# A two-layer hybrid trunk on one core: warm opening, low parts last, GpSimd for some low parts, another norm and pump order

## The chip, the cores and the metric

The kernel runs on one core of a Trainium2 chip, as one program. The metric is the device time of one execution in microseconds (us), and of several runs the median. Engines: PE (TensorE), whose matmuls bear the work; DVE (VectorE), ACT (ScalarE) and POOL (GpSimd) for work on elements; SP, which issues most DMAs. All of them run side by side, each through its own queue in order, and wait for each other through semaphores. TensorE's granted clock is given as a share of its full 2.4 GHz; the lower level is 1.2 GHz, shown as 0.50.

## The reference

Two layers over 256 positions of 1024 channels, all in float32, with a conditioning vector c that gives each layer shifts, scales and gates:

```python
for l in range(2):
    mod = silu(c) @ ada_w[l] + ada_b[l]           # 6 x 1024: shift, scale, gate, twice
    h = rmsnorm(x) * norm_mix * (1 + sc1) + sh1
    proj = h @ w_in[l]                            # one projection, split by columns
    # c_q, c_kv, k_rope | q, k, v, o, i, f of the mLSTM | two merge gates
    y_mla  = attention(rmsnorm(c_q) @ w_uq, rmsnorm(c_kv) @ w_ukv, rope)   # block-causal
    y_lstm = sigmoid(o) * headnorm(mlstm(silu(conv(q, k)), v, i, f))       # running maximum M
    x = x + g1 * ((sigmoid(g_a) * (y_mla @ w_bra) + sigmoid(g_l) * (y_lstm @ w_brl)) @ w_out)
    h = rmsnorm(x) * norm_ffn * (1 + sc2) + sh2
    a, v = split(conv3(h @ w_up))                 # 2816 channels each
    x = x + g2 * ((gelu(a) * v) @ w_down)
return rmsnorm(x) * final
```

## The kernel before

Activations lie with channels on the 128 partitions and the 256 positions along the free axis. A weight matrix is read in units, most of them 1024 x 256, and a unit in two pieces of 128 x 1024, each one DMA of 512 KB on SP's queue into `raw`. Float32 accuracy is reached by splitting: `_Weights.split` lets ACT copy a piece to the high part `whi` (fp32r) and DVE subtract it to get the low part `wlo`, and activations are split in the same way (`hh` and `hl`, `mh` and `ml`, `gh` and `gl`, `ua` and `ub`). A product is then three matmuls per 128 x 128 block of weights: high by high, high by low activation, low by high activation; `fm_steps` and `tm_steps` issue these three for each k in turn, and with `late_lo` all low weight parts of a slot behind the others.

The program is emitted unit by unit. A unit takes its weights with `W.take()`, which also loads further ones and queues the split of the next; `pair_slots` makes its four slots of 12 matmuls. Between slots `unit` advances side generators (evictions, norms, attention and mLSTM pieces, each yielding between its steps), emits one queued split piece, and, where a list of slots says so, a pump: `ada_block` reads 512 KB of ada_w on SP's queue and multiplies it on DVE by silu(c), summing along the row. So where a DVE operation stands in its queue is set by the slot at which it was emitted. The lists are `BRANCH_PUMPS` (units of the two branch projections), `OUT_PUMPS`, `UP_PUMPS` and `DOWN_PUMPS`; `NORM_AT` is the unit of the down projection at which the next layer's scales are put together. Each operation on ACT and DVE is also held back by `_Engine` until the one eight before it is emitted as done, so the order hardly shifts; all are recorded on one or two lines of its helper.

The stages of the trace, in us: the opening (0 to 52) with the first norm and the first six units of w_in's columns, block by block as x's blocks are normalised; the rest of the projection with the norms of c_q and c_kv, w_uq and w_ukv (to 115); attention and mLSTM between more units (to 178.5); the branch projections w_bra and w_brl (to 202.5), out (to 244), up (to 360), down (to 402), then the second layer the same way.

In the opening, GpSimd raises the mean square to the power −1/2 (`rs_cols`), `rs_tile` broadcasts it over partitions with matmuls and ACT copies it to `rs`, by which DVE multiplies x.

Of the kernel before, what the change touches and what calls it, by code (L numbers as in the profile page):

```python
# [19 lines left out]
P = 128  # L20
T = 256
# [39 lines left out]
BRANCH_PUMPS = (0, 2, 4, 6)  # L61
OUT_PUMPS = ((1, 2, 3, 4, 5), ())
UP_PUMPS = ((4, 6, 8), ())
DOWN_PUMPS = ((2, 2, 2, 2, 2, 1, 1, 1, 1, 1, 1), (1,) * 8)
NORM_AT = 11
# [6 lines left out]
MASK_SLOTS = (4, 3) + (2,) * 6  # L72
LATER = (2, 2, 2, 0)
# [5 lines left out]
class _Part:  # L79


    def __init__(self, nk, m):
        self.nk, self.m, self.cut, self.tiles = nk, m, (nk + 1) // 2, []
# [10 lines left out]
class _Weights:  # L94


    def __init__(self, nc, act, dve, raw, hi, lo, nm, ahead):
        self.act, self.dve = act, dve
# [5 lines left out]
    def add(self, src, nk, m):  # L104
        self.list.append((src, nk, m))
# [7 lines left out]
    def split(self, r):  # L113
# [5 lines left out]
        self.dve.tensor_tensor(l, r, h.bitcast(F32), ALU.subtract)  # L119
        return h, l  # L120

    def load_to(self, n):
        while self.loaded < min(n, len(self.list)):
            src, nk, m = self.list[self.loaded]
            part = _Part(nk, m)
            c0 = 0
            for i in range(2):
                c = part.cols(i)
                part.tiles.append(self.load(src[:, c0:c0 + c]))
                c0 += c  # L130
# [3 lines left out]
    def queue_split(self, n):  # L134
# [4 lines left out]
        src, nk, m = self.list[n]  # L139
# [3 lines left out]
        def piece(i):  # L143
            def emit():
                h, l = self.split(raw.tiles[i])
# [4 lines left out]
        self.pieces += [piece(0), piece(1)]  # L150
# [42 lines left out]
def hybrid_trunk(ctx, tc, a):  # L193
# [48 lines left out]
    W = _Weights(nc, act, dve, wraw, whi, wlo, nm, ahead=2)  # L242
# [48 lines left out]
    def tm_steps(out, w, h, ks, tb, csl, start=True, stop=True):  # L291
# [4 lines left out]
        for i, k in enumerate(ks):  # L296
# [4 lines left out]
            pe.matmul(out, hh[:, k, tsl], wl.at(k, csl), start=False, stop=last)  # L301
# [89 lines left out]
    dve.memset(minus_half, -0.5)  # L391
    halfpi = const.tile([P, 1], F32, name="halfpi")
# [114 lines left out]
    def norm_columns(n, l, wkey, sh, sc):  # L507
# [10 lines left out]
        for b in n.filled:  # L518
            u_fill(n, b)

# [37 lines left out]
    def norm_rest(n):  # L558
# [10 lines left out]
        for k0 in range(0, KB, 2):  # L569
# [10 lines left out]
            yield  # L580
# [26 lines left out]
    def mixer(l, n, begun):  # L607
# [26 lines left out]
        ats = sA.tile([8, T], F32, name=nm("ats"), tag="ats")  # L634
# [8 lines left out]
        def c_evict(i0, srcs):  # L643
# [5 lines left out]
            for i, src in enumerate(srcs):  # L649
                b = i0 + i  # L650
                gain = ppc(l, "qn", b) if b < 3 else ppc(l, "kvn", b - 3)
                if begun:
# [53 lines left out]
        def gates():  # L706
# [52 lines left out]
            dve.tensor_copy(ats, at[0:8, :T])  # L759
            dve.tensor_tensor_scan(M, ats, ats, 0.0, ALU.max, ALU.max)  # L760
# [234 lines left out]
        if begun:  # L995
# [7 lines left out]
            W.flush()  # L1003
            next(misc)
            for c in cs:
                next(c)
            sides.extend([conv, misc] + cs[1:] + cs[:1] + [widen()])
        else:
# [6 lines left out]
            slots, outs = pair_slots(W.take(), h, [bank()[:, :T], bank()[:, :T]])  # L1015
# [4 lines left out]
        for i in range(4):  # L1020
            if 3 + i not in first:
                slots, outs = pair_slots(W.take(), h, late_lo=bool(first) and i == 1)
# [24 lines left out]
        for hp in range(2):  # L1047
            b = bank()

            def slot(b=b, hp=hp):  # L1050
                for j in range(2):
                    fm_steps(b[:, j * T:(j + 1) * T], w, (ch[0], cl[0]), range(2),
                             slice((2 * hp + j) * P, (2 * hp + j + 1) * P), h0=3)
# [3 lines left out]
        for tb in range(2):  # L1057
            b = bank()

            def slot(b=b, tb=tb):  # L1060
                tm_steps(b, w, ckv, range(2), tb, slice(512, 1024))
# [104 lines left out]
    def ffn(l, fx, n):  # L1166
# [3 lines left out]
        def evict(j, srcs):  # L1170
# [6 lines left out]
            yield  # L1177
# [16 lines left out]
        for j in range(FB):  # L1194
# [5 lines left out]
            slots, outs = pair_slots(W.take(), h, [bank()[:, :T], bank()[:, :T]] if j == 2 else None)  # L1200
# [36 lines left out]
    for l in range(DEPTH):  # L1237
# [76 lines left out]
    normalised(slice(0, 1))  # L1314
    for k in range(KB):
# [11 lines left out]
        for dst in (h32, hh):  # L1327
# [178 lines left out]
```

## Time and profile before

| | before |
|---|---|
| runs | 814.19, 814.35 (the median), 817.71 us |
| the profiled execution, its own time | 819.43 us |
| its span in the trace | 817.6 us |
| busy: PE, DVE, ACT, GpSimd | 786.3, 687.1, 497.9, 91.7 us |
| bytes moved by DMA | 188.67 MB, 231 GB/s on the mean |

The span is the time from the first to the last event of the profiled execution, and its own time includes what lies around that. PE is close to always busy, so the reader should look less at the shares than at what fills the gaps in PE's row of the timeline, stage by stage. "128x1024" is partitions by elements; `wlo<-raw,whi` reads: the low part is written from raw and the high part. In the rows by stage the engines stand in the order PE, PEld (weight loads), DVE, ACT, POOL, each with its count of instructions. A bracket at the end of a timeline row is idle time of that engine just before the operation, and what ended it.

### The profile page before, as it was taken

How to read it: one execution, taken by the hardware profiler on the slowest of the kernel's cores; microseconds unless marked ns; L12 is line 12 of the kernel's file. 1: busy time of each engine (PE TensorE's matmuls, PEld its weight loads, DVE VectorE, ACT ScalarE, POOL GpSimd, SP SyncE). 2: the span in 40 equal slices, each digit the busy share in tenths (PEclk: the TensorE clock that was granted, in tenths of full speed). 3: DMA queues.
4: the chain of work that ended last, by engine and by line, in shares of the span. 5: the costliest groups of instructions: out<-in, count | busy, mean ns of one | idle time of the engine just before them, and what ended most of it. 6: DMA issues, size and time to landing. Idle time of an engine off the chain costs nothing. (4 is left out here: it accounts for less than half of the span.)

```text
span 817.6 us, 16692 instructions
## 1 busy us (share of the span) xinstructions
PE 786.3 (96%) x6416; PEld 769.2 (94%) x6416; DVE 687.1 (84%) x1244; ACT 497.9 (61%) x912; POOL 91.7 (11%) x118
## 2 busy tenths in 40 slices
PE   5999899999999999999899998999999999999995
PEld 4999789999899999999899998999999999999995
DVE  6979888789999988898968887788987988889742
ACT  5657658644577666643557584866366866665541
POOL 5801232000100000000101022100011000000010
PEclk7999999999999999999999998999999999999998
DMA  9986896788847755478876479677864565646841
GB/s 338 397 293 185 251 337 205 249 299 279 263 144 252 246 195 194 126 251 289 308 289 200 132 231 330 212 230 246 303 224 156 181 218 176 196 138 210 285 120 51
DMA packets 57712, 188.67 MB, mean 231 GB/s; under 512 B 6896, under 2 KB 8992, under 8 KB 57632
## 3 DMA queue, kind: packets, MB, share of 16 engines
q1 hardware_dynamic: 55520, 183.10, 66.6%
q0 software_dynamic: 1248, 2.28, 1.1%
q10 hardware_dynamic: 864, 2.23, 0.8%
q8 instruction: 50, 0.82, 0.4%
q14 instruction: 30, 0.25, 0.1%
HBM read 184.29 MB, written 1.06 MB: 227 GB/s over the span
## 5 line engine op out<-in xcount | busy, mean ns | idle before, releaser
L184 ACT CAST whi<-raw 128x1024 fp32r<-128x1024 f32 (+3 forms) x276 | 259.7, 950 | 120.0 <-PE bank L184 74.7
L184 DVE TENSOR_TENSOR wlo<-raw,whi 128x1024 fp32r<-128x1024 f32 (+3 forms) x276 | 304.5, 1109 | 26.4 <-PE bank L184 11.0
L184 PE MATMUL bank<-hh,whi 128*128 128x256 f32 x970 | 277.8, 287 | 0.0
L184 PE MATMUL bank<-hh,wlo 128*128 128x256 f32 x970 | 272.8, 282 | 1.1 <-DVE wlo L184 1.1
L184 PE MATMUL bank<-hl,whi 128*128 128x256 f32 x970 | 273.3, 282 | 0.0
L184 PEld LDWEIGHTS bank<-hh,wlo 128*128 128x128 f32 x970 | 183.7, 189 | 1.5 <-DVE wlo L184 1.5
L184 PEld LDWEIGHTS bank<-hh,whi 128*128 128x128 f32 x970 | 183.7, 189 | 1.1 <-issue 0.2
L184 PEld LDWEIGHTS bank<-hl,whi 128*128 128x128 f32 x970 | 183.8, 190 | 0.9 <-DVE hl L184 0.4
L184 DVE SCALAR_TENSOR_TENSOR ada<-ada,sact 128x1024 f32<-128x1024 f32 x96 | 117.7, 1230 | 19.6 <-DMA ada<-in_ada 19.4
L184 DVE SCALAR_TENSOR_TENSOR z<-bank,pp,z 128x255 f32<-128x255 f32 (+2 forms) x208 | 95.2, 477 | 19.8 <-ACT z L184 17.6
L184 PE MATMUL bank<-gh,wlo 128*128 128x256 f32 x352 | 99.2, 282 | 2.7 <-DVE wlo L184 2.6
L184 PE MATMUL bank<-gl,whi 128*128 128x256 f32 x352 | 99.1, 281 | 0.0
L184 PE MATMUL bank<-gh,whi 128*128 128x256 f32 x352 | 98.9, 281 | 0.0
L184 PEld LDWEIGHTS bank<-gh,wlo 128*128 128x128 f32 x352 | 66.3, 188 | 3.3 <-DVE wlo L184 3.3
L184 PEld LDWEIGHTS bank<-gh,whi 128*128 128x128 f32 x352 | 66.3, 188 | 0.0
L184 PEld LDWEIGHTS bank<-gl,whi 128*128 128x128 f32 x352 | 66.3, 188 | 0.0
L184 PE MATMUL bank<-ub,whi 128*128 128x256 f32 (+1 forms) x250 | 56.9, 282 | 0.0
L184 ACT ACTIVATE z<-bank,pp 128x256 f32<-128x256 f32 x96 | 49.0, 557 | 5.7 <-PE bank L184 3.9
L184 ACT ACTIVATE w<-z 128x256 f32<-128x256 f32 x60 | 24.9, 417 | 36.8 <-DVE z L184 35.3
L184 POOL TENSOR_TENSOR sqs<-sq,sq 128x256 f32<-128x256 f32 x4 | 3.2, 803 | 375.2 <-issue 281.6
L186 PE MATMUL bank<-hh,whi 128*128 128x256 f32 x150 | 44.3, 299 | 0.0
L184 PEld LDWEIGHTS bank<-ub,whi 128*128 128x128 f32 x250 | 42.8, 189 | 0.0
(254 smaller groups left out, 1409.1 us busy)
## 6 DMA issues: line engine op xcount, KB each, us to landing
ada<-in_ada SPq DMA_DIRECT2D x96, 512.0 KB, 5.1
raw<-in_w_up SPq DMA_DIRECT2D x88, 512.0 KB, 4.6
raw<-in_w_in SPq DMA_DIRECT2D x64, 512.0 KB, 5.0
raw<-in_w_down SPq DMA_DIRECT2D x32, 384.0 KB, 4.3
raw<-in_w_down SPq DMA_DIRECT2D x32, 320.0 KB, 3.5
raw<-in_w_out SPq DMA_DIRECT2D x16, 512.0 KB, 5.7
raw<-in_w_first SPq DMA_DIRECT2D x8, 512.0 KB, 8.3
raw<-in_w_bra SPq DMA_DIRECT2D x8, 512.0 KB, 4.9
```

The source lines that it names most:

```text
L184: r = f(*args, **kw)
L186: r = f(*args, **kw)
```

## The change

The change has these parts.

- Opening: the last DVE add over squares goes; the sum over partitions is now made of eight 128x128 matmuls instead of four 128x1, eleven idle matmuls (`keep_busy`, six and five) on a bank of their own stand around the broadcast matmuls, an early GpSimd power on ones (`warmp`) goes ahead, and the first block is multiplied straight from the bank, `rs` being copied later.
- Low parts last: `late_lo` also in `tm_steps`, in w_ukv's units, in all convolution units and one unit of out; `late_slots` orders the high parts of both column halves ahead of the low ones for a unit of the projection, one of up and the first of out.
- w_uqr is loaded and split in one piece; the scan of M reads its bank directly; four of five gain products of `c_evict` move from DVE to ACT.
- Pumps: `BRANCH_PUMPS`, `OUT_PUMPS` and `DOWN_PUMPS` get other slots, `NORM_AT` goes from 11 to 13, `norm_columns` fills u one block at a time (`catch_up`), `norm_rest` yields half as often, the evictions of the first unit of up wait longer.
- GpSimd works out the low part of every second piece of w_bra and w_brl in both layers, and of w_out in the first: twelve subtractions of 128x1024.

```diff
-BRANCH_PUMPS = (0, 2, 4, 6)
-OUT_PUMPS = ((1, 2, 3, 4, 5), ())
+BRANCH_PUMPS = (0, 1, 3, 4)
+OUT_PUMPS = ((1, 3, 5), ())
 UP_PUMPS = ((4, 6, 8), ())
-DOWN_PUMPS = ((2, 2, 2, 2, 2, 1, 1, 1, 1, 1, 1), (1,) * 8)
-NORM_AT = 11
+DOWN_PUMPS = ((1, 2, 1, 1, 2, 1, 1, 2, 2, 1, 1, 2, 1), (1,) * 8)
+NORM_AT = 13
...
+BUSY = (6, 5)
...
-        self.nk, self.m, self.cut, self.tiles = nk, m, (nk + 1) // 2, []
+        self.nk, self.m, self.cut, self.tiles = nk, m, nk if nk * m <= 1024 else (nk + 1) // 2, []
+        self.n = 1 + (self.cut < nk)
...
-    def split(self, r):
+    def split(self, r, eng=None):
...
         self.act.copy(h, r)
-        self.dve.tensor_tensor(l, r, h.bitcast(F32), ALU.subtract)
+        (eng or self.dve).tensor_tensor(l, r, h.bitcast(F32), ALU.subtract)
         return h, l
...
-                h, l = self.split(raw.tiles[i])
+                h, l = self.split(raw.tiles[i], self.gp if shared and i == 1 else None)
...
-        self.pieces += [piece(0), piece(1)]
+        self.pieces += [piece(i) for i in range(hi.n)]
...
-    def tm_steps(out, w, h, ks, tb, csl, start=True, stop=True):
...
             pe.matmul(out, hh[:, k, tsl], wh.at(k, csl), start=first, stop=False)
             pe.matmul(out, hl[:, k, tsl], wh.at(k, csl), start=False, stop=False)
-            pe.matmul(out, hh[:, k, tsl], wl.at(k, csl), start=False, stop=last)
+            if not late_lo:
+                pe.matmul(out, hh[:, k, tsl], wl.at(k, csl), start=False, stop=last)
+        for i, k in enumerate(ks):
+            if late_lo:
+                pe.matmul(out, hh[:, k, tsl], wl.at(k, csl), start=False, stop=stop and i == len(ks) - 1)
+
+    def late_slots(w, h, cut=KB):
+
+
+        outs = [bank()[:, :T], bank()[:, :T]]
+        todo = []
+        for ks in (range(cut), range(cut, KB)):
+            for parts in ((0, 1), (2,)):
+                todo += [(k, j, i) for k in ks for j in range(2) for i in parts]
+        ends = [max(n for n, (k, j, i) in enumerate(todo) if j == m) for m in range(2)]
+
+        def slot(n0):
+            def run():
+                for n in range(n0, n0 + 12):
+                    k, j, i = todo[n]
+                    pe.matmul(outs[j], w[i == 2].at(k, slice(j * P, (j + 1) * P)), h[i == 1][:, k, :],
+                              start=k + i == 0, stop=n in ends)
+            return run
+
+        return [slot(n0) for n0 in range(0, len(todo), 12)], outs
...
+    warmp = small(2)
+    gp.tensor_tensor(warmp, ones[:, 0:2], minus_half[:, 0:1].to_broadcast([P, 2]), ALU.pow)
...
-        for b in n.filled:
+        spawn(catch_up(n, sorted(n.filled)))
+
+    def catch_up(n, blocks):
+        for b in blocks:
             u_fill(n, b)
+            yield
...
-            yield
+            if k0 % 4 == 2:
+                yield
...
-                if begun:
+                if begun and i0 == 4:
                     dve.tensor_scalar(cc_[:, b, :], src, gain, None, ALU.mult)
                 else:
                     act.activation(cc_[:, b, :], src, AF.Copy, scale=gain)
...
             yield
-            dve.tensor_copy(ats, at[0:8, :T])
-            dve.tensor_tensor_scan(M, ats, ats, 0.0, ALU.max, ALU.max)
+            dve.tensor_tensor_scan(M, minus_half[0:8].to_broadcast([8, T]), at[0:8, :T], 0.0, ALU.max, ALU.max)
...
+            for c in cs[1:]:
+                next(c)
             next(misc)
-            for c in cs:
-                next(c)
+            next(cs[0])
...
-            slots, outs = pair_slots(W.take(), h, [bank()[:, :T], bank()[:, :T]])
+            slots, outs = late_slots(W.take(), h)
...
-                slots, outs = pair_slots(W.take(), h, late_lo=bool(first) and i == 1)
+                slots, outs = pair_slots(W.take(), h, late_lo=True)
...
-                             slice((2 * hp + j) * P, (2 * hp + j + 1) * P), h0=3)
+                             slice((2 * hp + j) * P, (2 * hp + j + 1) * P), h0=3, late_lo=True)
...
-                tm_steps(b, w, ckv, range(2), tb, slice(512, 1024))
+                tm_steps(b, w, ckv, range(2), tb, slice(512, 1024), late_lo=True)
...
-            slots, outs = pair_slots(W.take(), (mh, ml), split=(c in (0, 3)))
             if c == 0:
-                slots = [slots[0], slots[2], slots[1], slots[3]]
+                slots, outs = late_slots(W.take(), (mh, ml), 6)
+            else:
+                slots, outs = pair_slots(W.take(), (mh, ml), split=c == 3, late_lo=c == 1)
...
-            yield
+            for _ in range(3 if j == 0 else 1):
+                yield
...
-            slots, outs = pair_slots(W.take(), h, [bank()[:, :T], bank()[:, :T]] if j == 2 else None)
+            slots, outs = late_slots(W.take(), h) if j == 2 else pair_slots(W.take(), h)
...
-                W.add(a[k][l, c], 4, 512)
+                W.add(a[k][l, c], 4, 512, shared=True)
...
-            W.add(a["w_out"][l, c], KB, 256)
+            W.add(a["w_out"][l, c], KB, 256, shared=l == 0)
...
-    dve.tensor_tensor(sq[:, 0:2, :], sq[:, 0:2, :], sq[:, 4:6, :], ALU.add)
...
-    stat = bank()
-    for i in range(2):
+    stat, idle = bank(), bank()
+
+    def keep_busy(n):
+
+        for _ in range(n):
+            pe.matmul(idle[:, :P], ones, ones, start=True, stop=True)
+
+    for i in (0, 1, 4, 5):
         for tb in range(2):
-            pe.matmul(stat[:, tb:tb + 1], sq[:, i, tb * P:tb * P + P], ones[:, 0:1],
-                      start=i + tb == 0, stop=i + tb == 2)
+            pe.matmul(stat[:, tb * P:tb * P + P], sq[:, i, tb * P:tb * P + P], ones,
+                      start=i + tb == 0, stop=i + tb == 6)
...
-    y = rs_cols(stat)
+    y = rs_cols(stat[:, 0:T:P])
+    keep_busy(BUSY[0])
     ada_block(0, 0, ada0)
     rotary_angles()
-    rs = rs_tile(y)
+    bc = bcast_mm(y, 2)[:, :T]
+    keep_busy(BUSY[1])
+    dve.tensor_tensor(xr[:, 0, :], x[:, 0, :], bc, ALU.mult)
+    rs = work.tile([P, T], F32, name=nm("rs"), tag="rs", bufs=1)
...
-    normalised(slice(0, 1))
...
-        for dst in (h32, hh):
+        if k == 0:
+            act.activation(h32[:, k, :], xr[:, k, :], AF.Identity, bias=m0[:, k:k + 1], scale=m0[:, 8 + k:9 + k])
+            act.copy(rs, bc)
+        for dst in (h32, hh)[k == 0:]:
```

PE's instructions from the sum of squares to the first product of the projection (`act_c` is c spread out for `sact`, `ub` holds the squares, and its product with `ones` is the sum; `cst` by `sm` is the broadcast, `ua` by `raw` the first product). Before:

```order
L184 MATMUL bank_121<-cst,act_c 128x128 x3
L184 MATMUL bank_126<-cst,act_c 128x128 x4
L184 MATMUL bank_149<-ones,ub_137 128x1 x4
L184 MATMUL bank_209<-cst,sm_160 128x128 x2
L184 MATMUL bank_214<-ua_136,raw_227 128x256 x2
```

After:

```order
L187 MATMUL bank_128<-cst,act_c 128x128 x4
L187 MATMUL bank_150<-ones,ub_139 128x128 x8
L187 MATMUL bank_151<-ones 128x128 x6
L187 MATMUL bank_221<-cst,sm_166 128x128 x2
L187 MATMUL bank_151<-ones 128x128 x5
L187 MATMUL bank_231<-ua_138,raw_243 128x256 x2
```

The sum has eight matmuls instead of four, and the eleven by `ones` alone stand on both sides of the broadcast.

DVE's instructions in the first layer's branch projections (`ada` is a pump, `wlo` a low part, `ua` and `w` the merge). Before:

```order
L184 TENSOR_TENSOR wlo_2226<-raw_2115,whi_2225 128x1024
L184 SCALAR_TENSOR_TENSOR ada_2241,mod_84<-ada_2241,sact 128x1024
L184 TENSOR_TENSOR wlo_2277<-raw_2198,whi_2276 128x1024
L184 SCALAR_TENSOR_TENSOR ada_2280,mod_84<-ada_2280,sact 128x1024
L184 TENSOR_TENSOR wlo_2296<-raw_2200,whi_2295 128x1024
L184 SCALAR_TENSOR_TENSOR ua_1200<-ua_1200,bank_2274 128x2x256
L184 TENSOR_TENSOR wlo_2344<-raw_2270,whi_2343 128x1024
L184 SCALAR_TENSOR_TENSOR ua_1200<-ua_1200,bank_2311 128x2x256
L184 SCALAR_TENSOR_TENSOR ada_2347,mod_84<-ada_2347,sact 128x1024
L184 TENSOR_TENSOR wlo_2363<-raw_2272,whi_2362 128x1024
```

After:

```order
L187 SCALAR_TENSOR_TENSOR ada_2219,mod_84<-ada_2219,sact 128x1024
L187 SCALAR_TENSOR_TENSOR ada_2250,mod_84<-ada_2250,sact 128x1024
L187 TENSOR_TENSOR wlo_2286<-raw_2207,whi_2285 128x1024
L187 SCALAR_TENSOR_TENSOR ada_2289,mod_84<-ada_2289,sact 128x1024
L187 SCALAR_TENSOR_TENSOR ua_1209<-ua_1209,bank_2283 128x2x256
L187 SCALAR_TENSOR_TENSOR ada_2322,mod_84<-ada_2322,sact 128x1024
L187 TENSOR_TENSOR wlo_2356<-raw_2279,whi_2355 128x1024
L187 SCALAR_TENSOR_TENSOR ua_1209<-ua_1209,bank_2320 128x2x256
L187 SCALAR_TENSOR_TENSOR w_441_2388<-tgl_1211,bank_2353 128x512
```

Every second low part is gone from the row, and the pumps stand closer together. They stand in GpSimd's row now, where after two powers of the attention seven of the eight come in sequence before the first square of the next norm:

```order
L187 TENSOR_TENSOR sm_2082<-sm_2078,minus_half 128x8
L187 TENSOR_TENSOR wlo_2235<-raw_2124,whi_2234 128x1024
L187 TENSOR_TENSOR wlo_2305<-raw_2209,whi_2304 128x1024
L187 TENSOR_TENSOR wlo_2372<-raw_2281,whi_2371 128x1024
L187 TENSOR_TENSOR wlo_2451<-raw_2351,whi_2450 128x1024
L187 TENSOR_TENSOR wlo_2515<-raw_2422,whi_2514 128x1024
L187 TENSOR_TENSOR wlo_2595<-raw_2494,whi_2594 128x1024
L187 TENSOR_TENSOR wlo_2672<-raw_2569,whi_2671 128x1024
L187 TENSOR_TENSOR sqs_2665<-sq_2663,sq_2668 128x256
```

PE's instructions in a slot of w_ukv in the first layer, the two weight pieces mixed. Before:

```order
L186 MATMUL bank_1138<-ua_890,wlo_1094 128x256
L186 MATMUL bank_1138<-ua_890,whi_1070 128x256
L186 MATMUL bank_1138<-ub_891,whi_1070 128x256
L186 MATMUL bank_1138<-ua_890,wlo_1071 128x256
L186 MATMUL bank_1138<-ua_890,whi_1093 128x256
L186 MATMUL bank_1138<-ub_891,whi_1093 128x256
L186 MATMUL bank_1138<-ua_890,wlo_1094 128x256
L186 MATMUL bank_1157<-ua_890,wlo_1094 128x256
```

After:

```order
L189 MATMUL bank_1147<-ua_904,wlo_1104 128x256
L189 MATMUL bank_1147<-ua_904,whi_1080 128x256
L189 MATMUL bank_1147<-ub_905,whi_1080 128x256
L189 MATMUL bank_1147<-ua_904,whi_1103 128x256
L189 MATMUL bank_1147<-ub_905,whi_1103 128x256
L189 MATMUL bank_1147<-ua_904,wlo_1081 128x256
L189 MATMUL bank_1147<-ua_904,wlo_1104 128x256
```

In a slot the low parts are read in its last matmuls instead of in every third, ahead of the transposes of M.

## Rows read from the trace of the kernel before

**Rows 1.** By stage: window, length, busy by engine, clock, DMA share, GB/s.

```profile
15.20:22.70 7.50, 7.48 (x32) 6.76 (x33) 7.50 (x15) 5.65 (x13) 6.66 (x11) 0.60 1.03 406
22.70:52.00 29.30, 29.30 (x204) 27.80 (x203) 24.49 (x45) 17.17 (x37) 15.54 (x22) 1.00 1.01 375
52.00:95.00 43.00, 39.54 (x307) 36.70 (x305) 40.54 (x95) 31.77 (x56) 7.92 (x12) 1.00 0.71 217
...
178.50:202.50 24.00, 24.00 (x206) 24.00 (x205) 23.97 (x34) 9.77 (x11) 0.00 (x0) 1.00 0.87 296
202.50:228.40 25.90, 23.32 (x190) 22.51 (x190) 25.15 (x43) 13.89 (x25) 5.02 (x6) 1.00 0.84 261
228.40:244.00 15.60, 15.04 (x125) 14.66 (x124) 13.60 (x31) 12.70 (x27) 0.71 (x1) 1.00 0.39 132
...
360.00:402.00 42.00, 39.34 (x328) 38.73 (x327) 35.87 (x60) 18.14 (x30) 2.37 (x4) 1.00 0.89 311
...
505.84:512.66 6.82, 6.57 (x28) 6.42 (x29) 4.40 (x10) 2.76 (x7) 1.24 (x2) 0.50 0.85 273
...
580.00:626.00 46.00, 45.93 (x387) 45.69 (x386) 38.48 (x58) 24.77 (x42) 6.56 (x7) 1.00 0.66 223
...
sum 817.60, PE 786.25 PEld 769.20 DVE 687.05 ACT 497.86 POOL 91.68; mean PE 43.68 PEld 42.73 DVE 38.17 ACT 27.66 POOL 5.09
```

**Rows 2.** PE's waits: engine, line, releaser, total us, times, longest us.

```profile
PE bank L184 <- DVE wlo L184: 5.4, 6, 2.1
...
PE bank L186 <- DVE wlo L184: 2.6, 5, 1.6
...
PE bank L186 <- DVE M L184: 0.9, 1, 0.9
```

**Rows 3.** Timeline of the opening: start, us, engine, operation; in brackets idle before.

```profile
10.54 1.21 DVE L184 SCALAR_TENSOR_TENSOR ada<-ada,sact 128x1024 f32<-128x1024 f32 x1
...
10.71 1.62 POOL L186 TENSOR_TENSOR sm<-sm,minus_half 128x2 f32<-128x2 f32 x1 [7.59 <-DVE sm L184]
...
12.38 1.22 PE L184 MATMUL bank<-cst,sm 128*128 128x128 f32 x4 [1.96 <-POOL sm L186]
15.22 0.79 PE L184 MATMUL bank<-ua,raw 128*128 128x256 f32 x1 [1.62 <-ACT ua L184]
...
13.64 0.37 ACT L184 COPY rs<-bank 128x256 f32<-128x256 f32 x1 [3.93 <-PE bank L184]
...
22.09 1.37 DVE L184 TENSOR_TENSOR wlo<-raw,whi 128x512 fp32r<-128x512 f32 x2
...
24.67 0.29 PE L184 MATMUL bank<-hh,wlo 128*128 128x256 f32 x1
```

**Rows 4.** Operations by form: operation, count, busy us, mean ns, idle before.

```profile
L184 DVE TENSOR_TENSOR wlo<-raw,whi 128x1024 fp32r<-128x1024 f32 x190 | 233.0, 1229 | 9.3 <-ACT whi L184 3.3 <-PE bank L184 3.1 <-issue 2.5
...
L184 DVE TENSOR_SCALAR cqkv<-bank,pp 128x256 f32<-128x256 f32 x5 | 2.1, 477 | 0.5 <-ACT w L184 0.5
```

**Rows 5.** Timeline of DVE and POOL around two GpSimd products.

```profile
208.55 0.74 POOL L184 TENSOR_TENSOR sqs<-sq,sq 128x256 f32<-128x256 f32 x1 [47.06 <-ACT sq L184]
...
208.61 1.76 DVE L184 TENSOR_TENSOR wlo<-raw,whi 128x1024 fp32r<-128x1024 f32 x1
...
616.29 1.80 POOL L184 TENSOR_TENSOR sqs<-sqs,sq 128x256 f32<-128x256 f32 x1 [0.79 <-ACT sq L184]
...
616.27 1.22 DVE L184 TENSOR_TENSOR wlo<-raw,whi 128x1024 fp32r<-128x1024 f32 x1
617.41 0.48 DVE L184 SCALAR_TENSOR_TENSOR x<-bank,mod,x 128x256 f32<-128x256 f32 x1
```

**Rows 6.** Timeline of DVE and PE at the end of down.

```profile
399.13 1.22 DVE L184 SCALAR_TENSOR_TENSOR ada<-ada,sact 128x1024 f32<-128x1024 f32 x1 [0.88 <-DMA ada<-in_ada]
...
401.76 0.38 PE L184 MATMUL bank<-gh,wlo 128*128 128x256 f32 x1 [2.09 <-DVE wlo L184]
```

**Rows 7.** Timeline of PE in the second layer's mLSTM.

```profile
506.09 1.51 PE L184 MATMUL bank<-vaug,w 128*128 128x65 f32 x6 [2.15 <-DVE w L184]
```

More of the change, by code (lines that the diff above doesn't have):

```diff
@@ L94, with __init__ @@
 class _Weights:
-    def __init__(self, nc, act, dve, raw, hi, lo, nm, ahead):
-        self.act, self.dve = act, dve
+    def __init__(self, nc, act, dve, gp, raw, hi, lo, nm, ahead):
+        self.act, self.dve, self.gp = act, dve, gp
         self.nc, self.raw, self.hi, self.lo, self.nm, self.ahead = nc, raw, hi, lo, nm, ahead
@@ L102, in __init__, with add @@
         self.pieces = []
-    def add(self, src, nk, m):
-        self.list.append((src, nk, m))
+    def add(self, src, nk, m, shared=False):
+        self.list.append((src, nk, m, shared))
     def load(self, src):
@@ L123, in load_to @@
         while self.loaded < min(n, len(self.list)):
-            src, nk, m = self.list[self.loaded]
+            src, nk, m, _ = self.list[self.loaded]
             part = _Part(nk, m)
             c0 = 0
-            for i in range(2):
+            for i in range(part.n):
                 c = part.cols(i)
@@ L138, in queue_split @@
         self.load_to(n + 1)
-        src, nk, m = self.list[n]
+        src, nk, m, shared = self.list[n]
         raw = self.raws.pop(n)
@@ L239, in v2 @@
         return t.rearrange("p (n t) -> p n t", n=2)
-    W = _Weights(nc, act, dve, wraw, whi, wlo, nm, ahead=2)
+    W = _Weights(nc, act, dve, gp, wraw, whi, wlo, nm, ahead=2)
     sides = []
@@ L289, in fm_steps, with tm_steps @@
                 pe.matmul(out, wl.at(k, msl), hh[:, h0 + k, :], start=False, stop=stop and i == len(ks) - 1)
-    def tm_steps(out, w, h, ks, tb, csl, start=True, stop=True):
+    def tm_steps(out, w, h, ks, tb, csl, start=True, stop=True, late_lo=False):
         wh, wl = w
@@ L1287, in hybrid_trunk @@
         act.copy(sact[:, 128 * i:128 * i + 512], bcs[i // 4])
-    dve.tensor_tensor(sq[:, 0:2, :], sq[:, 0:2, :], sq[:, 4:6, :], ALU.add)
     act.activation(warm, warm, AF.Silu)
-    stat = bank()
-    for i in range(2):
+    stat, idle = bank(), bank()
[3 more added lines that the diff above has]
+    for i in (0, 1, 4, 5):
         for tb in range(2):
-            pe.matmul(stat[:, tb:tb + 1], sq[:, i, tb * P:tb * P + P], ones[:, 0:1],
-                      start=i + tb == 0, stop=i + tb == 2)
+            pe.matmul(stat[:, tb * P:tb * P + P], sq[:, i, tb * P:tb * P + P], ones,
+                      start=i + tb == 0, stop=i + tb == 6)
     dve.scalar_tensor_tensor(plus, pp[:, 0, ob + 8:ob + 16], 1.0, pp[:, 0, on:on + 8], ALU.add, ALU.mult)
```

1 line of the change is left out of this document (removed).

## Prediction

> **What bounds the kernel now.** I read the trace by stages first, then the waits of PE, then those waits in the timeline. The busy times by stage [rows 1] show PE busy for 786.25 of 817.60 us, so only the 31.35 us in which it stands still, and the stretches at the lower clock, can be won. Within the stages where the change works, PE idles 43.00 − 39.54 = 3.46 us from 52 to 95, 2.58 from 202.5 to 228.4, 0.56 from there to 244 and 2.66 from 360 to 402. What ends these idle times is mostly a low part that DVE brings late [rows 2]: 5.4 and 2.6 us in six and five waits, apart only because the helper issues matmuls from two lines; the scan M ends another 0.9. DVE is the reason: from 178.5 to 202.5 it is busy 23.97 of 24.00 us and from 202.5 to 228.4 25.15 of 25.90. Between these stages PE is gapless, and a gain of another engine there is worth nothing.
>
> The profiled execution took 819.43 us with a span of 817.60; the median of the runs is 814.35. Part of the 5.1 us between them has a row: from 505.84 to 512.66 TensorE had a granted clock of 0.50, its 1.2 GHz level, after it had stood 2.15 us for one late DVE operation [rows 1, 7]; at 2.4 GHz the 6.82 us would have been half as long, 3.4 us. So I sum against 819.43 − 3.4 = 816.0 and take the same difference off the median. The other 1.7 us I leave out on both sides.
>
> **The opening: −2.2 us (−3.0 to 0).** The power on GpSimd starts at 10.71 and takes 1.62 us, the broadcast matmuls start at 12.38, ACT copies their result at 13.64, and the first product of the projection starts at 15.22 [rows 3]. From 15.20 to 22.70 the clock is 0.60 on the mean, from 22.70 it is full [rows 1]. Three things change. x's first block is multiplied straight from the bank, so the copy (0.37, with the hand-over some 0.5) leaves the path. A DVE add over 512 columns leaves it too, about 0.7 us between the 0.477 of 256 and the 1.229 of 1024 [rows 4]; of the eight stat matmuls in its place half can run ahead, so I take 0.5. That is −1.0 whatever the clock. And eleven idle matmuls fill TensorE's waits for the power and the product: if the clock is then 2.4 GHz at 15, the first block's products shrink by over 3 us. Not all of it counts, because DVE feeds this stage: its low parts for the second block start at 22.09 (two, 1.37 together, so the first is there at 22.8) and PE takes it at 24.67 [rows 3]. That is 1.9 us of slack, so −2.9 at best, −3.0 with the whole add. I take −2.2, somewhat over half of the slack, since part of it will be eaten by transfers: the weights of 22.7 to 52 come at a DMA share of 1.01 [rows 1], and if they bound it all, nothing is gained (rival D). `warmp` is priced at nothing: the slow power began while DVE's ada product (10.54, 1.21) was under way and ended 0.58 behind its end, so a wait for the port explains its length, and a cold first use isn't needed for that.
>
> **First layer's norms, w_uq and w_ukv, 52 to 95: −3.0 us (−3.5 to 0).** DVE is busy 40.54 of 43.00 us there [rows 1]. Off it go four gain products of 0.477 [rows 4], the copy before the scan (0.4 by the same size of copy) and the second, overhead-laden piece of w_uqr (0.15): 1.9 + 0.4 + 0.15 = 2.5 us; ACT, with 31.77 of 43.00 busy, has room for the gains. Beside this the late low order pushes each unit's first need of a low part back by 8 to 16 matmuls, 1 to 2 us at 0.12 each, against the five waits of 2.6 us, the longest 1.6 [rows 2]. With M's 0.9 both together cover 3.5, which is all the idle time there is. −3.0 leaves one half-microsecond gap. What is late next is the scan, which reads the bank and still stands behind DVE's queue.
>
> **GpSimd's low parts, pumps and out, 178.5 to 244: +1.0 us (−3.1 to +6).** DVE is busy for 23.97 + 25.15 + 13.60 = 62.7 of 65.5 us. Eight low parts leave it at 1.229 less the 0.08 by which such operations overlap [rows 4], 9.1 us, and two of the five pumps in out, 1.2 each: 11.5 us off. Against this stand eight GpSimd operations of 128x1024. The trace has none. Its nearest row is a 128x256 product: 0.74 us alone, and a DVE low part that began beside it took 1.76 instead of 1.229, so 0.53 of blocking for 256 columns [rows 5]. Likewise the GpSimd one at 616.29 took 1.80 where a DVE low part had started first at 616.27, and the DVE operation at 617.41, which reads a bank, ran beside it in its 0.48. So each engine waits for the other's whole instruction, except DVE's operations on PSUM. Four times 0.53 is 2.1; I take 2.2 a piece (bounds 1.23, as fast as DVE, and 4 × 0.74 = 2.96). Eight give 17.6 us of blocking. Beside them DVE has eight 128x512 and eight 128x256 operations on banks (counted in the order of its instructions), at least 16 × 0.48 = 7.7 us, of which I count two thirds, 5.1, as cover. 17.6 − 5.1 − 11.5 = +1.0: DVE, which set the pace, gets a little more to do, and PE's loss there follows it. The lower end is the 2.58 + 0.56 that PE idles; the upper has no cover at all, 17.6 − 11.5. The waits now read GpSimd: behind each of its parts the next one is queued, and w_out's halves with late low order wait last. In the second layer four more parts move, but there DVE is busy only 38.48 of 46.00 us [rows 1], so 4 × (2.2 − 1.1) = 4.4 more fits: nothing.
>
> The Trainium skill's SBUF — State Buffer ("Who interferes with whom") says that a DVE operation with two SBUF inputs and a GpSimd operation reading SBUF exclude each other for a whole instruction; rows 5 agree, with 1.76 and 1.80. It speaks against this part of the change, and without it the stretch would give −3.1 instead of +1.0 (rival B). The Trainium skill's GPSIMD Engine Reference (section 3.1) has GpSimd's tensor_tensor 1.96 times slower than DVE's; no run here shows it yet, and with that estimate, 2.4 us a part, the stretch would be +2.6 and the whole 809.9.
>
> **Pumps in down, 360 to 402: −1.7 us (−2.6 to 0).** DVE waited 0.88 for ada's DMA at 399.13, its low part came behind that, and PE stood 2.09 us [rows 6]. Down's first five units had two pumps each; now eighteen are spread over thirteen units. The two moved from out cost 2.4 us of DVE here, but DVE is busy 35.87 of 42.00 and PE waits mostly for the order. The pumps' DMAs share SP's queue with the weights and are now issued more evenly at a share of 0.89. I take −1.7 of the 2.66.
>
> **Second layer, 504 to 506: −0.2 us (−2 to 0).** PE waits 2.15 us for w behind a pump [rows 7]; the new order puts other operations ahead of it, but the transposes that follow wait for the same DVE queue, and I let the wait pass on to them. NORM_AT, fewer yields in the norm, blockwise u and the delayed evict change the order where PE is gapless: nothing.
>
> **Sum.** −2.2 − 3.0 + 1.0 − 1.7 − 0.2 = −6.1, so 816.0 becomes 809.9 in a profiled execution without the slow stretch, and 814.35 becomes **808.2 us**.
>
> **Rivals.** B: GpSimd's parts cost nothing, because it runs while DVE works on banks or waits. For it: sixteen such operations; against it: 23.97 of 24.00. The stretch gives −3.1: 804.1. D: the opening and the first norms give back. For it: DMA share 1.01 behind the opening, and late low order only moves a low part that DVE makes no sooner. Opening 0 and norms −1.5: 811.9; this is also how it looks if the idle matmuls don't do what they are put there for. C, slower: a part takes 2.9 us, its upper bound, and nothing covers it; the out units then wait for GpSimd in a row. The stretch is 8b − 11.5 for b us a part: with b = 2.9 it is +11.7, and 4 × 1.8 = 7.2 uses up the second layer's 7.5 but for some 2 us through order. 814.35 − 7.1 + 11.7 + 2 = 820.9. It decides against the kernel at b = 2.3 without cover, and by over 0.5% at 2.6 to 2.8. Against it: 0.53 for 256 columns.
>
> **How the numbers follow.** Forecast 0.50, B 0.20, D 0.18, C 0.12. Half a per cent, 4.1 us, is about what a measurement can tell from no change: below 810.3 and above 818.4. Faster: 0.42 of the forecast's share, all of B, 0.03 of D: 0.65. Slower: 0.11 of C. Same is the rest, 0.24. All lower bounds together give −3.0 − 3.5 − 3.1 − 2.6 − 2 = −14.2, 800.1; D with the upper half of the middle's bound gives 811.9 + 4.1 = 816. Range 800 to 816, leaving out C and little else.
>
> **What would show it.** Right: the first projection product nearer 14.5 than 15.22 with a clock of 1.00 soon after; PE idle under 1 us in the stage of 52 to 95; GpSimd low parts of 2.0 to 2.5 us with DVE low parts of over 1.7 beside them; PE waits named for GpSimd's parts of about 3 to 4 us in all in branch and out; no 2 us gap in down. Wrong: GpSimd parts below 1.5 (B) or near 3 in a chain (C); a clock of 0.50 until 21 (D); a new stretch at 0.50 in the middle of the kernel, which alone would cost some 3 us.

## The result

The changed kernel takes 827.67 us in the median of four runs (825.86 to 830.05), the kernel before 814.27: a ratio of 1.0157, with an interval of 1.0119 to 1.0195. It is slower by 13.4 us, where 6.1 us faster was forecast, and the time lies outside the range of 800 to 816.

The profile after, its busy times first:

```profile
PE 791.1 (96%) x6446; PEld 772.4 (94%) x6446; DVE 694.4 (84%) x1223; ACT 498.6 (60%) x914; POOL 125.5 (15%) x131
```

Against [rows 1], GpSimd's 91.68 us have become 125.5, and DVE's 687.05 have grown to 694.4 although it has fewer instructions. To see where the time went, the same stages of the program are put side by side: here those of the kernel after, as window, length, busy PE, PEld, DVE, ACT, POOL, clock, DMA share and GB/s. They are, in order, the first layer's norms to w_ukv, its branch projections, out, up (behind the two units that begin it), down from its first to its last product, and the second layer's out. (In the trace ahead of the prediction down runs from 351.8 to 417.2, so the window of 360 to 402 that the prediction calls down lies inside it.)

```profile
54.80:99.30 44.50, 42.38 (x317) 40.25 (x316) 40.24 (x88) 32.09 (x58) 9.46 (x14) 0.92 0.74 226
181.90:199.85 17.95, 17.32 (x146) 17.11 (x145) 17.92 (x21) 6.43 (x8) 7.25 (x3) 1.00 0.88 295
199.85:230.10 30.25, 25.54 (x194) 24.23 (x193) 27.30 (x39) 15.89 (x26) 13.31 (x9) 0.94 0.68 219
243.00:359.20 116.20, 113.86 (x962) 113.24 (x961) 106.13 (x184) 79.25 (x132) 0.00 (x0) 1.00 0.59 191
359.20:423.00 63.80, 62.94 (x530) 62.54 (x529) 56.92 (x94) 31.86 (x51) 6.89 (x6) 1.00 0.88 311
596.40:623.30 26.90, 23.99 (x194) 22.98 (x193) 21.34 (x31) 15.29 (x25) 3.79 (x5) 1.00 0.58 195
```

And the same stages of the kernel before, from a second trace of it (`again`, below) whose span is 813.2 us. That trace is used from here on, since the one ahead of the prediction was some 4 us longer than most executions:

```profile
56.70:101.00 44.30, 40.83 (x317) 37.92 (x316) 41.19 (x94) 31.07 (x55) 7.95 (x12) 1.00 0.71 215
181.80:198.80 17.00, 17.00 (x146) 17.00 (x145) 16.96 (x26) 7.15 (x9) 0.00 (x0) 1.00 0.86 294
198.80:223.80 25.00, 23.70 (x194) 22.90 (x193) 24.96 (x42) 13.96 (x24) 3.41 (x5) 1.00 0.86 281
236.70:350.90 114.20, 113.64 (x962) 113.26 (x961) 105.25 (x186) 79.39 (x133) 0.00 (x0) 1.00 0.58 191
350.90:415.40 64.50, 62.99 (x530) 62.66 (x529) 56.73 (x89) 32.67 (x51) 6.24 (x6) 1.00 0.89 307
589.20:613.20 24.00, 23.07 (x194) 22.82 (x193) 20.21 (x31) 15.30 (x26) 4.93 (x6) 1.00 0.66 220
```

The branch is 0.95 us longer, out 5.25, up 2.0, down 0.7 shorter, the second layer's out 2.9 longer. In the first layer's branch and out together DVE was busy for 17.92 + 27.30 = 45.2 us after and 16.96 + 24.96 = 41.9 before: in out its share of the stage fell from all of it to 27.30 of 30.25. So something else than a lack of DVE time holds PE. PE's waits after name it:

```profile
PE bank L187 <- ACT mh L187: 5.1, 4, 2.2
...
PE bank L187 <- DVE wlo L187: 4.6, 7, 1.1
...
PE bank L187 <- ACT whi L187: 2.4, 2, 1.2
...
PE bank L189 <- DVE wlo L187: 2.1, 3, 1.2
```

In `again` the row for `mh`, the high part of the merged branches, is:

```profile
PE bank L184 <- ACT mh L184: 1.2, 2, 0.9
```

So matmuls of out wait 5.1 us for `mh` where they waited 1.2. The third row above stands for up. The timeline of POOL, DVE, ACT and PE between the first layer's branch and out shows how the first came about:

```profile
196.61 2.42 POOL L187 TENSOR_TENSOR wlo<-raw,whi 128x1024 fp32r<-128x1024 f32 x1 [3.43 <-ACT whi L187]
...
197.22 2.89 DVE L187 TENSOR_TENSOR wlo<-raw,whi 128x1024 fp32r<-128x1024 f32 x1
...
201.42 0.69 DVE L187 TENSOR_TENSOR w<-w,ua 128x512 f32<-128x512 f32 x1
...
202.14 0.62 ACT L187 CAST mh<-w 128x512 fp32r<-128x512 f32 x1 [4.72 <-DVE w L187]
...
202.81 0.38 PE L187 MATMUL bank<-mh,whi 128*128 128x256 f32 x1 [0.90 <-ACT mh L187]
...
203.84 3.02 POOL L187 TENSOR_TENSOR wlo<-raw,whi 128x1024 fp32r<-128x1024 f32 x1 [4.81 <-ACT whi L187]
...
205.25 2.15 DVE L187 TENSOR_TENSOR w<-w,ua 128x512 f32<-128x512 f32 x1
...
208.21 0.58 PE L187 MATMUL bank<-mh,whi 128*128 128x256 f32 x1 [2.15 <-ACT mh L187]
```

GpSimd works on a low part from 196.61 to 199.03. DVE's own low part begins at 197.22 and takes 2.89 us instead of 1.229 [rows 4]: it stands until GpSimd is through and then needs its 1.1 us. Behind it in DVE's queue stands the merge, so `w` comes late, ACT makes `mh` at 202.14, and PE waits for it. The same again at 205.25: `w`, an operation of 128x512, takes 2.15 us beside GpSimd's next part, and PE stands 2.15 us for the last `mh`.

### The profile page after: what moved, and what is told of

It is laid out like the page before. It is cut to its first block, busy times and chain, and to the rows that moved or that the text cites. A ratio compares the mean times of both kernels' runs of the same rounds, so it can differ in the third digit from the quotient of the medians.

```text
span 825.7 us, 16761 instructions
## 1 busy us (share of the span) xinstructions
PE 791.1 (96%) x6446; PEld 772.4 (94%) x6446; DVE 694.4 (84%) x1223; ACT 498.6 (60%) x914; POOL 125.5 (15%) x131
## 3 DMA queue, kind: packets, MB, share of 16 engines
HBM read 184.29 MB, written 1.06 MB: 224 GB/s over the span
## 5 line engine op out<-in xcount | busy, mean ns | idle before, releaser
L187 ACT CAST whi<-raw 128x1024 fp32r<-128x1024 f32 (+3 forms) x274 | 259.3, 956 | 125.5 <-PE bank L187 68.9
L187 PE MATMUL bank<-hh,whi 128*128 128x256 f32 x973 | 273.7, 286 | 2.4 <-ACT whi L187 2.4
L187 PE MATMUL bank<-hl,whi 128*128 128x256 f32 x974 | 269.1, 281 | 0.1
L187 PE MATMUL bank<-hh,wlo 128*128 128x256 f32 x974 | 259.2, 281 | 2.6 <-DVE wlo L187 2.4
L187 PEld LDWEIGHTS bank<-hh,wlo 128*128 128x128 f32 x974 | 177.0, 188 | 3.6 <-DVE wlo L187 3.6
L187 DVE SCALAR_TENSOR_TENSOR ada<-ada,sact 128x1024 f32<-128x1024 f32 x96 | 122.8, 1283 | 16.0 <-DMA ada<-in_ada 15.6
L189 PE MATMUL bank<-hh,whi 128*128 128x256 f32 x147 | 43.9, 308 | 0.0
```

The source lines that it names most:

```text
L187: r = f(*args, **kw)
L189: r = f(*args, **kw)
```

## The experiments

Two theories were put up first. Theory 1: `late_slots` calls for high parts and activations too early, since it takes the high parts of all k before any low part; out and up, where time was lost, are where it is used. Theory 2: GpSimd's low parts block DVE, and what stands behind the blocked operation in DVE's queue is late.

**again.** The kernel before without a change.

> The kernel before, once more, with nothing changed, for a trace without the half-clock stretch at 505.84 to 512.66. If that stretch is what made the first profiled execution slow, the span is near 817.6 - 3.4 = 814, and below 812.5 if the other 1.7 us were disturbance too. If the stretch belongs to the order of the program, it stands there again.

814.97 us, span 813.2, and no stretch at half the clock between the opening and the tail; nor does any row of products stand there at the 0.41 us apiece that they take at half the clock, against 0.28. The stretch at 505.84 [rows 1] thus does not come with every execution of the program; the first trace was some 4 us longer.

**no_late_slots.** The kernel after with this undone (and the same in up and in the second layer's third unit):

```diff
-            if c == 0:
-                slots, outs = late_slots(W.take(), (mh, ml), 6)
-            else:
-                slots, outs = pair_slots(W.take(), (mh, ml), split=c == 3, late_lo=c == 1)
+            slots, outs = pair_slots(W.take(), (mh, ml), split=(c in (0, 3)), late_lo=c == 1)
+            if c == 0:
+                slots = [slots[0], slots[2], slots[1], slots[3]]
```

> The kernel after, with only late_slots undone in its three places (the second layer's third projection unit, the first unit of out, the third of up), GpSimd's low parts and all the rest kept. Theory 1, high parts and activations are called for too early by late_slots: the trace of after lost about 4.0 and 3.8 us in the two out stages and 2.0 and 2.1 in the two up stages, so some 10 to 12 us come back: 816 to 818 us. Theory 2, GpSimd's low parts hold up DVE and the merge, and the order only shows it: 825 to 828 us, out still waits for mh.

826.2 us (1.0134 of before, 1.0105 to 1.0163). Theory 1 falls: out still waits for `mh`, 6.4 us in its trace, and up still for `whi`, 2.4.

```profile
PE bank L187 <- ACT mh L187: 6.4, 2, 3.8
```

**lows_on_dve.** The kernel after, all low parts on DVE:

```diff
-                W.add(a[k][l, c], 4, 512, shared=True)
+                W.add(a[k][l, c], 4, 512)
...
-            W.add(a["w_out"][l, c], KB, 256, shared=l == 0)
+            W.add(a["w_out"][l, c], KB, 256)
```

> The kernel after, with all twelve of GpSimd's low parts back on DVE and nothing else changed. Theory 1: only what is left of the branch stages comes back, and out's low parts burden DVE again: 824 to 829 us. Theory 2: GpSimd's parts are the cause, each blocking a DVE operation for 1.7 us: 813 to 818 us.

817.61 us (1.0027, 1.0006 to 1.0047): 10 us come back, though DVE has twelve more operations to do. Its stages of branch and out, and the second layer's out, are those of the kernel before within a microsecond:

```profile
181.20:198.90 17.70, 17.38 (x147) 17.18 (x146) 17.67 (x27) 6.63 (x9) 0.00 (x0) 1.00 0.90 307
198.90:223.10 24.20, 23.40 (x194) 22.80 (x193) 23.56 (x37) 15.47 (x26) 4.45 (x6) 1.00 0.76 253
588.90:613.00 24.10, 23.32 (x194) 22.71 (x193) 19.37 (x27) 15.12 (x25) 3.79 (x5) 1.00 0.58 193
```

**before_gp_lows.** The kernel before with GpSimd's twelve low parts alone (the lines of the diff in `_Weights`, `shared` among them, on the old program).

> The kernel before, with GpSimd's twelve low parts alone added. Theory 1: near no change, 813 to 817 us. Theory 2: 820 to 826 us.

832.75 us (1.021, 1.0166 to 1.0255), 18 us slower and beyond even theory 2's number. PE waits 8.0 us for `mh` there, without `late_slots`:

```profile
PE bank L184 <- ACT mh L184: 8.0, 4, 3.8
```

So this part of the change is enough to make the kernel slower, and the rest of the change softens it.

**l_spare.** Is it the blocking, or that a part which PE needs comes 1.2 us later from GpSimd than from DVE? Here DVE makes all low parts, and GpSimd does a subtraction of the same size beside ten of them, whose result nobody reads:

```diff
-        (eng or self.dve).tensor_tensor(l, r, h.bitcast(F32), ALU.subtract)
+        self.dve.tensor_tensor(l, r, h.bitcast(F32), ALU.subtract)
+        if eng and self.spare is not None:
+            self.gp.tensor_tensor(self.spare, self.other, h.bitcast(F32), ALU.subtract)
...
```

> The kernel after with all low parts on DVE (as in lows_on_dve, 817.6), and for ten of the twelve shared pieces a GpSimd subtraction of the same size beside them, of sact and the piece's high part into a dead tile that nobody reads. If the port is the cause, DVE's operations beside it stretch to 2.9 to 3.4 us as in the kernel after, and the time is 824 to 830 us. If what costs is that GpSimd brings a needed low part late, nothing waits for these and it is 816 to 819 us.

833.89 us (1.024, 1.0207 to 1.0273), above the 824 to 830 expected: 16.3 us more than `lows_on_dve` for work off every path. POOL, DVE and PE beside two of these operations:

```profile
189.09 2.41 POOL L189 TENSOR_TENSOR kall<-sact,whi 128x1024 f32<-128x1024 f32 x1 [7.04 <-ACT whi L189]
...
189.61 2.97 DVE L189 TENSOR_TENSOR wlo<-raw,whi 128x1024 fp32r<-128x1024 f32 x1
...
192.64 0.39 PE L189 MATMUL bank<-qm,wlo 128*128 128x256 f32 x1 [1.31 <-DVE wlo L189]
...
194.93 3.46 POOL L189 TENSOR_TENSOR kall<-sact,whi 128x1024 f32<-128x1024 f32 x1 [3.43 <-ACT whi L189]
...
194.93 1.21 DVE L189 TENSOR_TENSOR wlo<-raw,whi 128x1024 fp32r<-128x1024 f32 x1
...
196.20 0.39 PE L189 MATMUL bank<-qm,wlo 128*128 128x256 f32 x1 [2.58 <-DVE wlo L189]
```

From 189.09 to 191.50 GpSimd works, DVE's low part of 189.61 takes 2.97, and PE waits 1.31 for it. At 194.93 both begin; DVE goes first in its 1.21, and GpSimd's takes 3.46. For this low part PE waits 2.58, since it stood behind the blocked one in DVE's queue. In the kernel after, SP's loads also wait 11.6 us, in five waits, until GpSimd's low parts free `raw`; in `l_spare` no load waits for GpSimd, and it is slower still. Blocking alone is enough to cost what the change lost; what the lateness of GpSimd's own parts adds to it was not measured apart.

**l_evict_back, l_yield_back.** `lows_on_dve` still lost 3.6 us in each layer's up, so two suspects in the order of the norm were undone, one at a time:

```diff
-            for _ in range(3 if j == 0 else 1):
-                yield
+            yield
```

> lows_on_dve with the first up unit's eviction yielding once again instead of three times. up took 117.8 us in both layers there against 114.2 before, with two waits of 1.4 us for ACT's high parts while ACT stood in front of the table load of the first gelu. If the late eviction is what holds ACT's queue, both layers give back 2 to 3.5 us: 811 to 814 us. If it is the norm's fewer yields: 816 to 819 us.

811.22 us (0.9951, 0.9934 to 0.9968).

```diff
-            if k0 % 4 == 2:
-                yield
+            yield
```

> lows_on_dve with norm_rest yielding after every pair of blocks again. If the norm's burst on DVE and ACT is what delays up's high parts, both layers give back 2 to 3.5 us: 811 to 814 us. If it is the late first eviction: 816 to 819 us.

811.28 us (0.9958, 0.9943 to 0.9974). Either one gives the whole loss back, where one of the two was expected to. The rows of ACT's queue at the first gelu, in `lows_on_dve` and then in `l_evict_back`, and the two waits of PE in the kernel after show why:

The first gelu's table load and the cast behind it in `lows_on_dve`, whose up begins at 236.0:

```profile
240.02 1.28 ACT L187 ACT_TABLE_LOAD   x1 [1.89 <-DVE z L187]
...
243.72 1.04 ACT L187 CAST whi<-raw 128x1024 fp32r<-128x1024 f32 x1
```

In `l_evict_back`, whose up begins at 234.6:

```profile
237.50 1.28 ACT L187 ACT_TABLE_LOAD   x1 [0.77 <-DVE z L187]
...
239.12 1.03 ACT L187 CAST whi<-raw 128x1024 fp32r<-128x1024 f32 x1
```

PE in up in the kernel after:

```profile
251.83 0.39 PE L187 MATMUL bank<-hh,whi 128*128 128x256 f32 x1 [1.18 <-ACT whi L187]
...
253.39 0.39 PE L187 MATMUL bank<-hh,wlo 128*128 128x256 f32 x1 [1.06 <-DVE wlo L187]
```

The table load and the first gelu, delayed by two more slots, stand in ACT's queue until DVE has made z; behind them, and in `lows_on_dve` behind four operations for the next blocks (241.64 to 243.52) as well, the casts to `whi` wait, and PE waits 1.18 for one of these and 1.06 for the low part that follows from it. That needs both: the late gelu, and a norm that emits twice as much for DVE and ACT at one slot. In `lows_on_dve` PE has the same two waits, of 1.2 and 1.06, in each layer's up, and its clock stands at half behind them:

```profile
247.00:250.40 3.40, 3.40 (x18) 3.40 (x18) 3.40 (x7) 2.12 (x3) 0.00 (x0) 0.51 0.56 176
```

The second layer has the like from 636.2 to 639.6. That is why up is 3.6 us longer there and only 2.0 in the kernel after, whose clock is 1.00 in up. So about half of what the order of the norm costs in the trace of `lows_on_dve` is the wait, and half the clock that fell behind it.

Each of these two kernels is faster than both the kernel before and the kernel after, and none of the later ones was faster still.

**l_no_late_slots.** `lows_on_dve` without `late_slots`.

> lows_on_dve with late_slots undone in its three places as well. If late_slots helps once DVE makes the low parts, 819 to 822 us; if it costs by asking early for high parts and activations, 812 to 815 us; with no_late_slots at 826.2 against 827.7 I expect within 2 us of 817.6.

817.17 us (1.0037, 1.0015 to 1.0058): `late_slots` is worth nothing either way once DVE makes the low parts.

**after_evict_back.** The kernel after with the one `yield` back, GpSimd's parts kept.

> The kernel after, GpSimd's low parts kept, with the first up unit's eviction yielding once again. If the late eviction and GpSimd's parts cost side by side, it loses the same as between lows_on_dve and l_evict_back, 6.4 us: 820 to 823 us. If the one only shows through the other: 825 to 828 us.

820.47 us (1.0079, 1.0048 to 1.011). 7.2 us come back, as 6.4 did without GpSimd's parts, so the two losses stand side by side, and 9.3 us stay between this and `l_evict_back`. (The runs come from three rounds, in each of which the kernel before was run again; its medians there are 814.82, 814.63 and 815.41, so differences between rounds are uncertain by up to about 1 us. Taken against the kernel before of their own round, the two are 8.5 us apart.)

**e_no_busy.** `l_evict_back` with `BUSY = (0, 0)`.

> l_evict_back (811.2) without the eleven idle matmuls. The first product there starts at 14.2 with a full clock, but the first stage then waits three times for weights of 33 to 45 us. If the transfers set the end of that stage, nothing is lost: 810 to 812 us. If the clock was worth the 1.2 us that the prediction put on it: 812 to 813 us.

811.9 us (0.9968, 0.9951 to 0.9984), no difference that can be told. The first stage of the projection in `e_no_busy` and in `l_evict_back`, in the columns of the stages above:

```profile
14.00:54.80 40.80, 40.77 (x265) 38.31 (x265) 35.40 (x66) 25.99 (x57) 22.74 (x35) 0.93 1.01 384
```

and

```profile
14.20:54.70 40.50, 38.76 (x264) 36.07 (x264) 35.09 (x65) 25.71 (x56) 22.81 (x35) 1.00 1.01 384
```

Without the idle matmuls the clock is lower and PE has no gap; with them the clock is full and PE idles 40.50 − 38.76 = 1.74 us. Both end within 0.1 us, at the same 384 GB/s.

**e_old_pumps.** `l_evict_back` with `BRANCH_PUMPS`, `OUT_PUMPS`, `DOWN_PUMPS` and `NORM_AT` of before.

> l_evict_back with the pumps of branch, out and down and NORM_AT as they were before. If the pumps' places win the 1.7 us forecast for down: 812.5 to 814 us, with the 1.8 us wait in down back. If the new places win nothing: 810.5 to 812 us.

813.34 us (0.9974, 0.9955 to 0.9992): 2.1 us more than `l_evict_back`, 1.3 when each is taken against the kernel before of its own round, and the intervals overlap. So a gain by the new places is likely but not shown. The wait of 1.8 us in down, expected back, did not come back; PE stands only this long there:

```profile
401.31 0.38 PE L187 MATMUL bank<-gh,wlo 128*128 128x256 f32 x1 [0.35 <-DVE wlo L187]
```

**e_norm_all_back.** `lows_on_dve` with the eviction's and the norm's yields as before and u filled in one go instead of by `catch_up`.

> lows_on_dve with all three changes to the norm's order undone (the eviction's yields, norm_rest's yields, u filled in one go). Either of the first two alone gave 811.2. If both relieve the same wait: 810 to 812 us. If they add: 806 to 808 us.

816.26 us (1.0024, 0.9999 to 1.0048), outside both expectations. It differs from `l_evict_back` in `norm_rest`'s yields and in u. In down, PE waits where it does not in `l_evict_back`, behind fillings of u that now stand in a row in DVE's queue:

```profile
403.83 0.47 DVE L187 SCALAR_TENSOR_TENSOR ub<-x,am,ua 128x256 fp32r<-128x256 f32 x1
...
404.23 2.55 DVE L187 TENSOR_TENSOR wlo<-raw,whi 128x768 fp32r<-128x768 f32 x3
...
405.23 0.39 PE L187 MATMUL bank<-gh,wlo 128*128 128x256 f32 x1 [1.86 <-DVE wlo L187]
```

The clock falls to half behind that wait, from 406.2 to 409.6. The wait and the half clock make 1.86 + 1.7 = 3.6 us, the medians differ by 5.0. So one block at a time seems worth some 3 to 5 us here, which I had priced at nothing; a run with the yields as before and u still block by block, which would show it alone, was not made.

## Why the prediction was wrong

The medians take the change apart. GpSimd's low parts cost 827.67 − 817.61 = 10.1 us, or 9.3 by the pair of `after_evict_back` and `l_evict_back`. The order of the norm costs 6.4 (817.61 to 811.22) or 7.2. What is left gains 814.63 − 811.22 = 3.4. The means, 9.7 + 6.8 − 3.4, make 13.1 of the 13.4 us. That the parts close is no evidence of its own, since both ways lead from 827.67 to 811.22; the 0.3 left over lies between two medians of the kernel before.

**GpSimd's parts: the step that failed.** The price of an operation was close: 2.2 us was taken for one of 128x1024, and alone it takes 2.40 to 2.44. The Trainium skill's GPSIMD Engine Reference (section 3.1) has a factor of 1.96; the estimate of 2.4 us from it agrees with the traces to the second digit. That each engine waits for the other's whole instruction held too, from both sides, 2.89 for DVE and 3.46 for GpSimd; the Trainium skill's SBUF — State Buffer ("Who interferes with whom") agrees. Even the net of DVE's load came out near the sum: from the branch to the third unit of up (the 45.2 and 41.9 us above, and 8.87 and 10.90 in the 12.9 us behind out) it was busy 54.1 us after and 52.8 before, +1.3 where +1.0 stood (partly by luck, since seven low parts and one pump less stand in this stretch, not eight and two). What failed is the sentence "PE's loss there follows it". Priced at +1.0, the stretch became 0.95 + 5.25 = 6.2 us longer. PE does not wait for DVE's load but for one operation in DVE's queue. A low part that DVE makes ahead of need was replaced by a stall of 1.7 us at a place that the start of GpSimd's instruction chose, and ahead of the merge that PE needs next. Cover did not help PE for the same reason: the operation on a bank stands in the queue behind the blocked one. The second layer, where I said that 4.4 us fit into DVE's idle time, lost 0.8 in the branch and 2.9 in out with four such parts. Rival C named the direction, but with 820.9 us, by a price of 2.9 us a part and from b = 2.6; the loss came at 2.4 and was 6.8 us larger, because the model of DVE's load was the wrong one.

**The order of the norm: priced at nothing.** "NORM_AT, fewer yields in the norm, blockwise u and the delayed evict change the order where PE is gapless: nothing" was the other failed step. In a stage where PE is gapless, a change of order can still make a gap: up lost some 2 us in the kernel after, 3.6 in `lows_on_dve` with the half clock behind the wait, in each layer. Blockwise u was by all signs not nothing either, but a gain.

**The opening: −2.2 forecast, the mechanism half right.** PE's rows in the opening after, and POOL's power and `warmp` ahead of it:

```profile
3.24 0.74 POOL L189 TENSOR_TENSOR sm<-ones,minus_half 128x2 f32<-128x2 f32 x1
...
10.49 1.61 POOL L187 TENSOR_TENSOR sm<-sm,minus_half 128x2 f32<-128x2 f32 x1 [6.50 <-DVE sm L187]
...
12.15 0.71 PE L187 MATMUL bank<-cst,sm 128*128 128x128 f32 x4 [0.60 <-POOL sm L187]
...
14.19 1.97 PE L187 MATMUL bank<-ua,raw 128*128 128x256 f32 x8 [0.21 <-DMA raw<-in_w_first]
...
34.52 1.97 PE L187 MATMUL bank<-ua,raw 128*128 128x256 f32 x8 [0.72 <-DMA raw<-in_w_first]
...
44.55 1.75 PE L187 MATMUL bank<-ua,raw 128*128 128x256 f32 x7 [0.64 <-DMA raw<-in_w_first]
```

The first product starts at 14.19 (15.22 in [rows 3], 16.46 in `again`), the clock is full, as forecast. In the kernel before the clock was at half there: the first eight products take 3.78 us in both of its traces, against 1.97 here, although the clock record of `again` reads 1.00 and so lacks that stretch. But PE then waits 0.72 and 0.64 for w_first, and the stage ends 1 us earlier than in the first trace and 2 us earlier than in `again`: the shift of the start, and nothing of the 1.9 us of slack. Rival D had the reason, the DMA share of 1.01, though it left no gain at all, and `e_no_busy` shows that the idle matmuls give nothing. `warmp` was priced right: 0.74 for it, and the power still takes 1.61.

**52 to 95: −3.0 forecast, −1.9 shown.** The stage takes 42.4 us in `lows_on_dve` against 44.3 (54.3 to 96.7 and 56.7 to 101.0). No wait for M stands among PE's waits after, as said, but the waits for low parts are 2.1 us in three instead of 2.6 in five [rows 2], so the low parts at the end of a slot took away 0.5 us of 2.6. In the kernel after even that is lost, since the clock stands at half for two stretches there, 0.92 on the mean, at some 1.7 us each.

**Down: −1.7 forecast.** 64.5 to 63.8 us after, 62.3 in `lows_on_dve` and `l_evict_back`: the size is near, but the cause is not shown to be the pumps. With the old pumps PE waits 0.35 us in down (`e_old_pumps`), with the new ones and u filled in one go 1.86 (`e_norm_all_back`), so the gap near its end goes with `catch_up` rather than with the pumps, which I had not seen. `l_yield_back`, with both new, still has one of 1.28 at 388.9, so what holds down open is not settled. **504 to 506: −0.2 forecast.** From the mLSTM's first score products to its fourth group of value products the second layer takes 24.4 us in `again` (496.04 to 520.45), 23.0 after and 23.7 in `l_evict_back`: the wait did not pass on whole.

## What to carry to other kernels

Before work goes to an engine whose instructions block those of the one in front, don't sum the load of both: ask which operation will stand in the second half of that long instruction, and who waits for the next three behind it in the queue. A stall of 1.7 us at a place that nobody chooses costs more than 1.2 us of work at a place that was chosen. And a change of order in a gapless stage needs a price too: look at which casts stand behind the operation that is made to wait.

## What the hardware showed beyond what I expected

TensorE's clock fell to its 1.2 GHz level in the middle of the kernel after some waits of about 2 us. Two such stretches of the kernel after, in the columns of the stages, and the wait ahead of the first:

```profile
116.03:119.45 3.42, 3.42 (x17) 3.25 (x15) 3.40 (x9) 0.92 (x4) 0.00 (x0) 0.50 0.79 231
208.19:211.61 3.42, 3.25 (x13) 2.96 (x14) 3.17 (x6) 1.65 (x2) 0.00 (x0) 0.50 0.56 168
...
115.62 1.29 PE L189 MATMUL bank<-kall,qall 128*128 128x128 f32 x4 [1.96 <-DVE w L187]
```

PE stood for 1.96 us there, and 2.15 us before the second, by the last row of the timeline between branch and out. Such a stretch of 3.4 us at half the clock costs 1.7 us beside the wait itself, so a wait of 2 us can cost nearly 4. It does not always: in `again` PE stood as long, and the clock stayed at 1.00.

```profile
504.12 0.85 PE L184 MATMUL bank<-vaug,w 128*128 128x65 f32 x6 [1.97 <-DVE w L184]
```

Nor is one long wait needed: in the kernel after, the clock also fell at 58, behind sixteen matmuls of one column without a wait, and at 88.8, behind waits of 0.64 and 1.25. Which stretches stand in a trace differs between kernels whose instructions there are the same: from 52 to 101 us there are two in the kernel after, one in `l_evict_back` and none in `lows_on_dve`. Single runs of one kernel lie up to 9 us apart (812.34 to 821.04 for `e_norm_all_back`). In `lows_on_dve` the time goes with the granted clock: four runs with 0.994 to 0.996 took 814.61 to 815.27 us, six with 0.988 to 0.990 took 816.87 to 819.93. In `e_norm_all_back` it hardly does (0.992 at both 812.34 and 818.86), so the clock is not the only reason.
